# Second staging buffer for the expert-weight matrices, taken from the gather buffers and from the resident chunks

## Chip, core and metric

The kernel runs on one core of one Trainium2 chip. The metric is device microseconds (us) of one execution. All inputs, outputs and spilled intermediates lie in the chip's HBM; the work is fp32, in part split into two fp32r pieces that are multiplied separately.

## What is computed

One layer of a streaming encoder for 1024 prompt tokens and 64 sample tokens (with 512 cached positions for the latter). The part that matters here is the last one, a PEER layer with 16384 single-neuron experts. Each token picks 128 experts (8 heads of 16); `u` and `v` are tables of 16384 rows of 1024 floats:

```python
def peer_tokens(h, w_q, keys, u, v):
    q = (h @ w_q).reshape(T, PEER_HEADS, 2, PEER_D_KEY // 2)
    s = jnp.einsum('thcd,hcnd->thcn', q, keys)
    s1, i1 = lax.top_k(s[:, :, 0], PEER_TOPK)
    s2, i2 = lax.top_k(s[:, :, 1], PEER_TOPK)
    ...
    top, sel = lax.top_k(cand, PEER_TOPK)
    idx = jnp.take_along_axis(cidx, sel, axis=-1)
    g = jax.nn.softmax(top, axis=-1)
    act = jax.nn.gelu(jnp.einsum('td,thkd->thk', h, u[idx]), approximate=False)
    return jnp.einsum('thk,thkd->td', g * act, v[idx])
```

Ahead of it stand one wide projection, differential attention (8 heads), latent attention (16 heads), the branch projections and an output projection.

## The kernel before

The 1088 tokens are nine tiles of 128 (tile 8 holds the 64 sample tokens). Three groups of three tiles (`GROUPS`) go through projections and attention one after the other: group 0 from 0 to about 760 us of the profiled execution, group 1 to about 1865 us, group 2 to about 2960 us. After that comes a last stage without projections, up to the end.

The experts' work of a group runs beside the next group's projections and attention, in four kinds of jobs, written as Python generators:

- `route_job` (VectorE, mostly) finds the 128 experts of each token of a tile.
- `dots_job` fetches, for k = 0 to 127, row `u[idx[token, k]]` for all 128 tokens with one indirect DMA that GpSimd issues (L333, 512 KB into a tile of 4 KB per partition), and VectorE multiplies it with the token's row and sums (L358). These are the gathers; six tiles of 128 gathers each, 768 in all, run beside groups 1 and 2, and 320 in the last stage.
- `build_job` (tiles 0 to 6) turns indices and weights of a tile into a dense matrix of 128 tokens by 16384 experts. For 8 tokens at a time VectorE makes one-hot rows (L402, L403) and products (L411), ScalarE makes one product (L408), TensorE multiplies them (L418, into a PSUM tile "mm" that the projections use too, two buffers), and ScalarE copies 4 tokens' result out of PSUM into `stage` (L424). `stage` holds 16 tokens, 8 KB per partition, so four copies fill it; one DMA of 1 MB, issued on SyncE's queue (`ld`, L69, called at L426), then writes it to the tensor `Ad` in HBM. There is one buffer of that tile, in the pool `bp`: the next copy into it waits until that DMA has landed.
- `vgather_job` (tiles 8 and 7) gathers rows of `v` instead of using a dense matrix (192 gathers, L453), at the very end.

The last stage multiplies the dense matrices with the whole table `v` (L1206 and L1221) in two passes, tiles 0 to 2 and tiles 3 to 6, reading `Ad` back as `araw` in 16 chunks per tile. Of tile 6 (`TR`) the first `RC` = 9 chunks are never written to `Ad`: ScalarE copies them to the resident tile `Ares` (L422), and only the other 7 go through `stage`. Before that, `Ares` serves as scratch of the routing.

The order: `pump(us)` is called in the projections and attention with the time that the work just issued is thought to take, and advances the three queues of jobs at set rates ("r" route, "d" dots, "b" build; a dense build advances 4 tokens per step at `RATE_B` = 0.3 steps per us). This gives the program order; the scheduler of the tile framework then orders each engine's instructions by that priority on a simulated timeline, and places the semaphore waits. `behind` keeps the product of a gather (L358, L453) from being placed ahead of the VectorE instruction that preceded it in program order. Each engine executes its own list in order.

Gather buffers: the pool `gp` has `NGB` = 4 (tag "gb"). While `cur["more"]` is set, which is in groups 1 and 2 alone, three of every seven gathers go to another pool, `gm`, with three buffers, so that seven gathers can be on their way; in the last stage there are four. The pool `gm` also holds a small tile `cq`. In the last stage `cur["p2"]` is the pool for nearly everything, with `Ares` in it.

Of the kernel before, what the change touches and what calls it, by code (L numbers as in the profile page):

```python
# [10 lines left out]
F32 = mybir.dt.float32  # L11
# [9 lines left out]
D = 1024  # L21
# [19 lines left out]
NGB = 4  # L41
PB = 5
NB = 8
RC = 9
NWHOLE = 8
TR = 6
RATE_R2 = 0.41
# [12 lines left out]
def hybrid_tile(ctx: ExitStack, tc: tile.TileContext, A):  # L60
# [3 lines left out]
    def ld(out, in_):  # L64
        if out.dtype == F32R:
            out = out.bitcast(F32)
        if in_.dtype == F32R:
            in_ = in_.bitcast(F32)
        return SP.dma_start(out, in_)  # L69
# [34 lines left out]
    bp = ctx.enter_context(tc.tile_pool(name="bp", bufs=1))  # L104
# [9 lines left out]
    cur = {"gp": gp, "sm": sm, "ps": ps_mm, "more": None}  # L114
    gturn = [0]
# [207 lines left out]
    def drain(q, key=None):  # L323
        while key not in done and advance(q):
            pass

    def gather(src, idx):
        gturn[0] += 1
        if cur["more"] and gturn[0] % 7 % 2:
            gb = cur["more"].tile([128, D], F32, name="gm", tag="gm")  # L330
        else:
            gb = cur["gp"].tile([128, D], F32, name="gb", tag="gb")
        G.indirect_dma_start(out=gb, out_offset=None, in_=src, in_offset=bass.IndirectOffsetOnAxis(ap=idx, axis=0))  # L333
        return gb
# [4 lines left out]
    def dots_job(t):  # L339
        if t in GROUPS[-1]:  # L340
            drain("r", ("route", t))
        ns = 128 if t < 8 else 64
        eidx = bp.tile([128, 128], I32, name="beidx")
        gk = bp.tile([128, 128], F32, name="bgk", tag="bgk")
        h2 = bp.tile([128, D], F32, name="h2r")
        if t < 8:
            ld(eidx, eidxd[t])
            ld(gk, gkd[t])
            ld(h2, h2d[t * 128:t * 128 + 128])
        else:  # L350
            ld(eidx[:, :64], packed(eidxd[8]))
            ld(gk[:, :64], packed(gkd[8]))
            src = h2d[NP:]
            ld(h2, bass.AP(tensor=src.tensor, offset=src.offset, ap=[[0, 2], [D, 64], [1, D]]))
        act = bp.tile([128, 128], F32, name="act")
        for k in range(ns):
            gb = gather(A["peer_u"], eidx[:, k:k + 1])
            behind(V.scalar_tensor_tensor(gb, gb, 1.0, h2, op0=ALU.mult, op1=ALU.mult, accum_out=act[:, k:k + 1]))  # L358
            yield
        wgt = act  # L360
        S.activation(wgt[:, :ns], act[:, :ns], AF.Gelu)
        V.tensor_tensor(wgt[:, :ns], wgt[:, :ns], gk[:, :ns], op=ALU.mult)
        ld(wgtd[t, :, :ns], wgt[:, :ns])
        if t not in VGATHER:
            queues["b"].append((("build", t), build_job(t)))

    def build_job(t):
        if t == TR:
            drain("r")
        src = bp.tile([128, 3, 128], F32, name="bsrc", tag="oh1")  # L370
        ld(src[:, 0, :], wgtd[t])
        ld(src[:, 1:3, :], efd[t])
        p = cur["ps"].tile([128, 512], F32, name="mm")
        pv = p.rearrange("p (a n) -> p a n", n=128)
        for i in range(3):
            PE.transpose(pv[:, i, :], src[:, i, :], ident)
        ixT = bp.tile([128, 2, 128], BF16, name="ixT")
        S.copy(ixT, pv[:, 1:3, :])
        aT = bp.tile([128, 128], F32, name="aT")
        S.copy(aT, pv[:, 0, :])  # L380
        a3 = bp.tile([128, 3, 128], BF16, name="a3")
        a3f = bp.tile([128, 128], F32, name="a3f")
        for i in range(3):
            V.tensor_copy(a3[:, i], aT)
            if i == 0:
                V.tensor_copy(a3f, a3[:, 0])
            if i < 2:
                V.tensor_tensor(aT, aT, a3[:, i], op=ALU.subtract)
        yield
        shp = [128, 4, 128, 2]  # L390
        iv = iota2[:, None, :, :].to_broadcast(shp)

        def over(row, tt):
            return row[:, tt:tt + 8].rearrange("p (g x) -> p g x", x=2)[:, :, None, :].to_broadcast(shp)

        n = RC if t == TR else 0
        for t0 in range(0, 128, 16):
            stage = bp.tile([128, 16, 4, 8, 4], F32, name="stage", tag="stage")
            for tt in range(t0, t0 + 16, 8):
                oh1 = bp.tile(shp, BF16, name="oh1", tag="oh1")  # L400
                oh2 = bp.tile(shp, BF16, name="oh2")
                V.tensor_tensor(oh1, iv, over(ixT[:, 1], tt), op=ALU.is_equal)  # L402
                V.tensor_tensor(oh2, iv, over(ixT[:, 0], tt), op=ALU.is_equal)  # L403
                w3 = bp.tile([128, 3] + shp[1:], BF16, name="w3")
                for i in range(3):
                    if i == 0:
                        for x in range(8):
                            S.activation(w3[:, 0, x // 2, :, x % 2], oh2[:, x // 2, :, x % 2], AF.Copy,  # L408
                                         scale=a3f[:, tt + x:tt + x + 1])
                    else:  # L410
                        V.tensor_tensor(w3[:, i], oh2, over(a3[:, i], tt), op=ALU.mult)  # L411
                for q in range(2):
                    p = cur["ps"].tile([128, 512], F32, name="mm")
                    pv = p.rearrange("p (a n) -> p a n", n=128)
                    for j in range(4):
                        x = 4 * q + j
                        for i in range(3):
                            PE.matmul(pv[:, j, :], lhsT=oh1[:, x // 2, :, x % 2], rhs=w3[:, i, x // 2, :, x % 2],  # L418
                                      start=i == 0, stop=i == 2)
                    pc = p.rearrange("p (t c i) -> p c i t", t=4, i=8)  # L420
                    if n:
                        S.copy(cur["Ares"][:, :, (tt + 4 * q) // 4], pc[:, :n])  # L422
                    if n < 16:
                        S.copy(stage[:, n:, (tt - t0) // 4 + q], pc[:, n:])  # L424
                    yield
            ld(Ad[t, :, n:, t0 // 4:t0 // 4 + 4], stage[:, n:])  # L426
# [9 lines left out]
    def vgather_job(t):  # L436
        while "p2" not in cur:
            yield
        ns = 128 if t < 8 else 64
        eidx = bp.tile([128, 128], I32, name="beidx")  # L440
        wgt = bp.tile([128, 128], F32, name="vwgt", tag="bgk")
        acc = cur["p2"].tile([128, D], F32, name="gacc", bufs=1)
        if t < 8:
            ld(eidx, eidxd[t])
            ld(acc, x1d[t * 128:t * 128 + 128])
        else:
            ld(eidx[:, :64], packed(eidxd[8]))
            V.memset(acc[64:128], 0.0)
            ld(acc[0:64], x1d[NP:])
        ld(wgt[:, :ns], wgtd[t, :, :ns])  # L450
        for k in range(ns):
            gb = gather(A["peer_v"], eidx[:, k:k + 1])
            behind(V.scalar_tensor_tensor(acc, gb, wgt[:, k:k + 1], acc, op0=ALU.mult, op1=ALU.add))  # L453
            yield
        if t == 8:
            oth = cur["gp"].tile([128, D], F32, name="gb", tag="gb")
            ld(oth[0:64], acc[64:128])
            V.tensor_tensor(acc[0:64], acc[0:64], oth[0:64], op=ALU.add)
        if t == VGATHER[-1]:
            cur["late"] = lambda: finish(acc, tr(t), t)  # L460
        else:
            finish(acc, tr(t), t)
# [675 lines left out]
    p2 = ctx.enter_context(tc.tile_pool(name="p2", bufs=2, reuse_waits="tile"))  # L1138
    cur["p2"] = cur["sm"] = p2
    Ares = p2.tile([128, RC, 32, 8, 4], F32, name="Ares", bufs=1)  # L1140
    Af = Ares.rearrange("p c q i t -> p (c q i t)")
# [24 lines left out]
    for ip, tiles in enumerate(PASSES):  # L1166
# [11 lines left out]
        for c in range(16):  # L1178
# [15 lines left out]
            for t in tiles:  # L1194
                if t == TR and c < RC:
                    raw = Ares[:, c]
# [141 lines left out]
```

## Time and profile before

| | before |
|---|---|
| time, median of 3 runs | 4510.65 us (4497.69 to 4512.42) |
| profiled execution: its time | 4499.18 us |
| profiled execution: span from first to last instruction | 4497.4 us |
| TensorE busy | 3847.6 us (86%) |
| VectorE busy | 3203.9 us (71%) |
| ScalarE busy | 1603.3 us (36%) |
| GpSimd busy | 1942.8 us (43%) |
| DMA | 1183.10 MB, mean 263 GB/s |

How to read the rows below. PE is TensorE's matmuls, PEld its weight loads, DVE VectorE, ACT ScalarE, POOL GpSimd, SP SyncE (SPq its queue of DMAs). `gb<-in_peer_u` is a gather; L333 is a line of the kernel. In a view of stretches a row is one stretch: its bounds, its length, then busy time and number of instructions of PE, PEld, DVE, ACT and POOL, TensorE's granted clock as a share of full speed, the mean busy share of the 16 DMA engines, and GB/s; the last row sums the stretches. In a view of waits a row says which instruction's engine stood idle until what: us in total, times, longest. In a timeline a row is start, length, engine, line, operation, tiles, count, and in brackets the idle time before it and what ended it. In the chain of work that ended last, a piece is start, length and what it is; a DMA's piece runs from its issue to the end of the wait for its landing.

### The profile page before, as it was taken

What the parts mean: (1) busy time and instruction counts of PE and PEld (TensorE: products, weight loads), DVE (VectorE), ACT (ScalarE), POOL (GpSimd) and SP (SyncE); (2) the same over time, 40 slices, a digit from 0 to 9 for tenths busy, and PEclk for the clock granted to TensorE, in tenths of its full rate; (3) what the DMA queues carried; (4) which work ended last, traced back from release to release, by engine and by line L of the source; (5) the groups of instructions that cost most, each with busy time, mean ns of one, the idle gap of its engine ahead of it and who ended that gap; (6) DMA issues with size and microseconds to landing.
All of it is one profiled execution on the core that took longest, in us unless ns stands there. A gap on an engine that the chain in (4) does not pass through costs nothing.

```text
span 4497.4 us, 55226 instructions
## 1 busy us (share of the span) xinstructions
PE 3847.6 (86%) x18633; PEld 2898.2 (64%) x18633; DVE 3203.9 (71%) x7136; ACT 1603.3 (36%) x3656; POOL 1942.8 (43%) x1353
## 2 busy tenths in 40 slices
PE   6998988898788798887868877889999969999991
PEld 6977887556565565655546666654457858888881
DVE  4043457977788767797786777659847987777776
ACT  3344622025455513322454455133113532232320
POOL 3412241554456441143444656513434445545455
PEclk9967999987898898998778888989999979999995
DMA  5421244996777785697776767988868999989987
GB/s 176 168 96 56 67 170 169 352 350 231 267 263 269 272 320 216 226 329 290 245 248 239 256 239 253 351 291 311 320 246 317 349 328 332 351 312 352 321 314 260
DMA packets 467587, 1183.10 MB, mean 263 GB/s; under 512 B 45352, under 2 KB 218888, under 8 KB 452584
## 3 DMA queue, kind: packets, MB, share of 16 engines
q0 software_dynamic: 184320, 671.17, 41.4%
q1 hardware_dynamic: 282984, 508.41, 32.3%
q8 instruction: 147, 2.41, 0.2%
q14 instruction: 136, 1.11, 0.1%
HBM read 1074.60 MB, written 104.56 MB: 262 GB/s over the span
## 4 chain that ended last, share of the span: by engine, by line
PE 42%; DMA 13%; DVE 13%; issue 5%; ACT 4%; POOL 2%; SPq 0%; another core or an unknown queue 0%; ACTq 0%; POOLq 0%; DVEq 0%
PE acc_ps L1221 16%; PE mm L167 9%; PE acc_ps L1206 5%; DMA Ad<-stage 4%; DMA gb<-in_peer_v,beidx 3%; DVE gb L358 3%; DMA gb<-in_peer_u,beidx 2%; PE mm L418 2%; DVE gm L358 2%; POOL gb L333 2%; PE mm L827 2%; PE sc L795 1%; PE mm L952 1%; PE sc L793 1%; ACT w L408 1%
## 5 line engine op out<-in xcount | busy, mean ns | idle before, releaser
L333 POOL DMA_INDIRECT gb<-in_peer_u,beidx x758 | 1028.2, 1356 | 1364.7 <-DVE gb L358 811.1
L358 DVE SCALAR_TENSOR_TENSOR gb<-gb,h2r 128x1024 f32<-128x1024 f32 x758 | 918.3, 1220 | 174.4 <-DMA gb<-in_peer_u,beidx 157.9
L333 POOL DMA_INDIRECT gm<-in_peer_u,beidx x330 | 429.9, 1303 | 501.4 <-DVE gm L358 274.6
L1221 PE MATMUL acc_ps<-vhi,ahi 128*128 128x512 f32 x1408 | 439.9, 395 | 23.4 <-ACT ahi L1214 23.4
L1221 PE MATMUL acc_ps<-vhi,alo 128*128 128x512 f32 x1408 | 444.1, 396 | 3.0 <-DVE alo L1215 3.0
L1221 PE MATMUL acc_ps<-vlo,ahi 128*128 128x512 f32 x1408 | 441.0, 395 | 0.0
L358 DVE SCALAR_TENSOR_TENSOR gm<-gm,h2r 128x1024 f32<-128x1024 f32 x330 | 402.1, 1218 | 24.0 <-DMA gm<-in_peer_u,beidx 21.4
L333 POOL DMA_INDIRECT gb<-in_peer_v,beidx x192 | 268.0, 1396 | 229.7 <-DVE gacc L453 150.1
L167 PE MATMUL mm<-h,wraw 128*128 128x384 f32 (+1 forms) x1024 | 325.5, 479 | 20.4 <-ACT qd L739 10.4
L1206 PE MATMUL acc_ps<-vw,aw 128*128 128x512 f32 x768 | 335.0, 596 | 1.4 <-ACT aw L1202 1.4
L418 PE MATMUL mm<-w,oh 128*128 128x128 bf16 x2688 | 231.0, 237 | 111.5 <-DVE oh L402 50.5
L1221 PEld LDWEIGHTS acc_ps<-vhi,ahi 128*128 128x128 f32 x1408 | 265.6, 189 | 85.5 <-ACT ahi L1214 23.6
L453 DVE SCALAR_TENSOR_TENSOR gacc<-gb,vwgt,gacc 128x1024 f32<-128x1024 f32 x192 | 246.2, 1282 | 93.3 <-DMA gb<-in_peer_v,beidx 88.1
L1221 PEld LDWEIGHTS acc_ps<-vhi,alo 128*128 128x128 f32 x1408 | 265.0, 189 | 63.9 <-DVE alo L1215 3.7
L1221 PEld LDWEIGHTS acc_ps<-vlo,ahi 128*128 128x128 f32 x1408 | 265.5, 189 | 60.2 <-DVE vlo L1192 0.2
L408 ACT ACTIVATE w<-oh,a3f 128x128 bf16<-128x128 bf16 x896 | 280.8, 429 | 54.0 <-DVE oh L403 24.3
L179 POOL TENSOR_TENSOR wlo<-wraw,whi 128x2048 fp32r<-128x2048 f32 (+1 forms) x42 | 186.8, 4447 | 260.6 <-ACT whi L178 255.0
L418 PEld LDWEIGHTS <-oh 128*128 128x128 bf16 x2688 | 191.9, 106 | 160.6 <-issue 73.2
L167 PEld LDWEIGHTS mm<-h,wraw 128*128 128x128 f32 x1024 | 201.0, 199 | 133.8 <-issue 11.4
L167 PE MATMUL mm<-wraw,h 128*128 128x256 f32 (+1 forms) x960 | 235.6, 402 | 37.7 <-ACT vt L720 27.8
L1206 PEld LDWEIGHTS acc_ps<-vw,aw 128*128 128x128 f32 x768 | 145.5, 191 | 179.1 <-issue 175.6
L1214 ACT CAST ahi<-araw 128x1024 fp32r<-128x1024 f32 x79 | 82.8, 1049 | 474.4 <-PE acc_ps L1221 395.7
(384 smaller groups left out, 7574.2 us busy)
## 6 DMA issues: line engine op xcount, KB each, us to landing
vraw<-in_peer_v SPq DMA_DIRECT2D x192, 512.0 KB
wraw<-in_w_in SPq DMA_DIRECT2D x66, 1024.0 KB
araw<-Ad SPq DMA_DIRECT2D x103, 512.0 KB
Ad<-stage SPq DMA_DIRECT2D x48, 1024.0 KB
vw<-in_peer_v SPq DMA_DIRECT2D x64, 512.0 KB
wraw<-in_w_a SPq DMA_DIRECT2D x12, 1024.0 KB
wraw<-in_w_b SPq DMA_DIRECT2D x12, 1024.0 KB
wraw<-in_w_out SPq DMA_DIRECT2D x12, 1024.0 KB
```

The costliest lines, as they stand in the source:

```text
L167: PE.matmul(out, lhsT=L[0], rhs=R[0], start=start, stop=stop)
L179: G.tensor_tensor(lo[:, :n], raw[:, :n], hi[:, :n].bitcast(F32), op=ALU.subtract)
L333: G.indirect_dma_start(out=gb, out_offset=None, in_=src, in_offset=bass.IndirectOffsetOnAxis(ap=idx, axis=0))
L358: behind(V.scalar_tensor_tensor(gb, gb, 1.0, h2, op0=ALU.mult, op1=ALU.mult, accum_out=act[:, k:k + 1]))
L408: S.activation(w3[:, 0, x // 2, :, x % 2], oh2[:, x // 2, :, x % 2], AF.Copy, scale=a3f[:, tt + x:tt + x + 1])
L418: PE.matmul(pv[:, j, :], lhsT=oh1[:, x // 2, :, x % 2], rhs=w3[:, i, x // 2, :, x % 2], start=i == 0, stop=i == 2)
L453: behind(V.scalar_tensor_tensor(acc, gb, wgt[:, k:k + 1], acc, op0=ALU.mult, op1=ALU.add))
L793: PE.matmul(ps[:nq, a:b], lhsT=Q[:, c, qc:qc + nq], rhs=K[:, c, a - o:b - o], start=True, stop=False)
L827: PE.matmul(po[:nq, :128], lhsT=PT[:kw, b, :nq], rhs=Vt[:kw, b, :], start=b == 0, stop=b == nb - 1)
L1206: PE.matmul(pst[t][:, ds], lhsT=rv[:, i, :], rhs=vb[i][:, ds], start=c == 0 and i == 0, stop=False)
L1214: S.copy(av, rv)
L1221: PE.matmul(pst[t][:, ds], lhsT=L[:, i, :], rhs=R[:, ds], start=c == (0 if ip else NWHOLE and -1) and i == 0 and L is ahi and R is vb[i][0 ...
```

## The change

The matrices' `stage` tile gets a second buffer of 16 tokens: every other block of 16 tokens is staged in a tile of the pool `gm` (in groups 1 and 2) or of the pool `p2` (in the last stage), the others in `bp` as before, each pool with one buffer. Its 8 KB per partition are found by leaving one gather buffer in `gm` instead of three (each 4 KB), so that five gathers instead of seven can be on their way in groups 1 and 2, one of five going to `gm`; and in `p2` by keeping 7 chunks of tile 6 resident instead of 9 (each 4 KB).

```diff
-RC = 9
+RC = 7
...
     def gather(src, idx):
         gturn[0] += 1
-        if cur["more"] and gturn[0] % 7 % 2:
-            gb = cur["more"].tile([128, D], F32, name="gm", tag="gm")
+        if cur["more"] and gturn[0] % 5 == 1:
+            gb = cur["more"].tile([128, D], F32, name="gm", tag="gm", bufs=1)
         else:
             gb = cur["gp"].tile([128, D], F32, name="gb", tag="gb")
...
         n = RC if t == TR else 0
         for t0 in range(0, 128, 16):
-            stage = bp.tile([128, 16, 4, 8, 4], F32, name="stage", tag="stage")
+            sp = (cur["more"] or cur["p2"]) if t0 % 32 else bp
+            stage = sp.tile([128, 16, 4, 8, 4], F32, name="stage", tag="stage", bufs=1)
```

## Rows read from the trace of the kernel before

**Rows 1.** The page's first part: busy time, share of the span, instructions

```profile
PE 3847.6 (86%) x18633; PEld 2898.2 (64%) x18633; DVE 3203.9 (71%) x7136; ACT 1603.3 (36%) x3656; POOL 1942.8 (43%) x1353
```

**Rows 2.** Groups 1 and 2, stretches 760 to 1865 and 1865 to 2960 us: their sum

```profile
sum 2200.00, PE 1798.61 PEld 1303.29 DVE 1706.54 ACT 848.90 POOL 1022.99; mean PE 899.30 PEld 651.65 DVE 853.27 ACT 424.45 POOL 511.50
```

**Rows 3.** Waits from 760 to 2960 us

```profile
POOL gb L333 <- DVE gb L358: 437.8, 100, 39.9
POOL gm L333 <- DVE gm L358: 274.6, 61, 18.5
...
ACT stage L424 <- DMA Ad<-stage: 130.2, 28, 15.4
ACT stage L424 <- PE mm L418: 116.6, 62, 7.9
```

**Rows 4.** The chain of work that ended last, 760 to 2960 us, by line

```profile
by line: PE mm L167 19.0%; DMA Ad<-stage 7.5%; issue 7.0%; DVE gb L358 5.7%; DVE gm L358 3.9%; PE mm L827 3.4%; PE mm L418 2.9%; PE sc L795 2.8%; PE mm L952 2.5%; PE sc L793 2.4%; DMA gb<-in_peer_u,beidx 2.3%; ACT w L408 2.1%; PE tp L758 1.
```

**Rows 5.** SyncE's timeline: issues of two stage DMAs of one build

```profile
1170.69 0.52 SPq L69 DMA_DIRECT2D Ad<-stage  x1
1202.35 0.53 SPq L69 DMA_DIRECT2D Ad<-stage  x1
```

**Rows 6.** TensorE's timeline, 1198 to 1240 us

```profile
1220.77 1.44 PE L418 MATMUL mm<-w,oh 128*128 128x128 bf16 x12 [7.59 <-ACT stage L424]
```

**Rows 7.** 29 stretches in which ACT waits for a stage DMA, to 2960 us

```profile
1204.71:1220.13 15.42, 8.47 (x36) 4.93 (x35) 9.69 (x17) 0.00 (x1) 8.04 (x7) 0.84 1.04 389
...
sum 135.13, PE 76.36 PEld 53.77 DVE 96.04 ACT 0.07 POOL 58.92; mean PE 2.63 PEld 1.85 DVE 3.31 ACT 0.00 POOL 2.03
```

**Rows 8.** The 8 us behind each of those 29 stretches

```profile
sum 232.00, PE 191.60 PEld 140.60 DVE 142.24 ACT 126.42 POOL 80.80; mean PE 6.61 PEld 4.85 DVE 4.90 ACT 4.36 POOL 2.79
```

**Rows 9.** Pieces of the chain in groups 1 and 2

```profile
1202.35 17.68 DMA Ad<-stage
...
2581.39 6.04 DMA gm<-in_peer_u,beidx
...
2836.74 19.43 DMA gm<-in_peer_u,beidx
```

**Rows 10.** Line L358, 760 to 2960 us: instructions, and idle time before them

```profile
L358 DVE SCALAR_TENSOR_TENSOR gb<-gb,h2r x438: 1199/1218/1344, 768.7 to 2945.8; 128x1024 f32<-128x1024 f32 x146
...
L358 DVE SCALAR_TENSOR_TENSOR gm<-gm,h2r x330: 1175/1218/1348, 766.3 to 2947.0; 128x1024 f32<-128x1024 f32 x165
...
  DMA gb<-in_peer_u,beidx: 40.0, 33
  DMA gm<-in_peer_u,beidx: 21.4, 24
```

**Rows 11.** Line L358, 3130 to 4000 us, likewise

```profile
L358 DVE SCALAR_TENSOR_TENSOR gb<-gb,h2r x297: 1197/1219/1349, 3130.5 to 3991.4; 128x1024 f32<-128x1024 f32 x149
...
  DMA gb<-in_peer_u,beidx: 111.6, 87
```

**Rows 12.** Line L453, likewise

```profile
L453 DVE SCALAR_TENSOR_TENSOR gacc<-gb,vwgt,gacc 128x1024 f32<-128x1024 f32 x192 | 246.2, 1282 | 93.3 <-DMA gb<-in_peer_v,beidx 88.1
```

**Rows 13.** 59 stretches in which DVE waits for a gather, 760 to 2960 us

```profile
sum 62.74, PE 51.70 PEld 34.85 DVE 0.15 ACT 11.76 POOL 40.19; mean PE 0.88 PEld 0.59 DVE 0.00 ACT 0.20 POOL 0.68
```

**Rows 14.** DMA issues of the page: count and size

```profile
araw<-Ad SPq DMA_DIRECT2D x103, 512.0 KB
...
Ad<-stage SPq DMA_DIRECT2D x8, 448.0 KB
```

**Rows 15.** Stage waits from 2960 to 3130 us

```profile
  DMA Ad<-stage: 33.3, 3
```

**Rows 16.** Stretches of the last stage

```profile
2960.00:3130.00 170.00, 154.95 (x617) 82.33 (x616) 135.24 (x582) 61.16 (x149) 32.27 (x27) 0.90 0.83 289
3660.00:3990.00 330.00, 304.71 (x1302) 246.86 (x1303) 251.30 (x372) 83.04 (x82) 179.77 (x129) 0.95 0.90 331
4400.00:4450.00 50.00, 0.00 (x0) 0.00 (x0) 35.42 (x56) 2.30 (x4) 27.95 (x23) 0.53 0.82 279
```

## The prediction

> **What bounds the kernel now.** The page comes first: TensorE is the busiest engine at 86% [rows 1], so what is to be gained lies where TensorE stands still and something else decides. The stretches of groups 1 and 2 show it: over 2200 us TensorE is busy 1798.61 us, 81.8%, while VectorE has 1706.54 us [rows 2]. No engine is full there; each waits for another in turn. In the last stage TensorE is nearer its limit (304.71 of 330 us in one stretch [rows 16]), and from 4400 us on it has no work at all: the end is a run of gathers of `v` with their products on VectorE [rows 16].
>
> The waits of groups 1 and 2 are read next. ScalarE stands 130.2 us, 28 times, before a copy into `stage` until the stage's previous contents have landed in HBM [rows 3]. The reader should see that this wait stands in an in-order queue: evictions of projections, exponentials and the copies of transposes are queued behind that copy. The chain of work that ended last gives the stage's DMA 7.5% of these 2200 us, 165 us, as the second largest line [rows 4]. A place shows how: the third DMA of a build was issued at 1202.35 [rows 5], landed 17.68 us later [rows 9], ScalarE waited 15.42 us of it [rows 7], and TensorE, whose "mm" buffers were both full, 7.59 us [rows 6].
>
> **The gain, step by step.** With two buffers, block n waits for the DMA of block n-2. Two issues in a row stand 31.66 us apart (1170.69 and 1202.35 [rows 5]); the landing took 17.68 us there, and that is among the longest waits. So a DMA has landed before its buffer is wanted again, and I take the 28 waits as gone. What is late next in their place is the copy's own input: 62 times ScalarE already waits for TensorE's L418 (116.6 us [rows 3]), since these matmuls are queued among the projections'. That wait stays.
>
> What the end gets from it is not ScalarE's 130 us but TensorE's loss. I cut the trace into the 29 stretches in which ScalarE waits so (135.13 us together; the view of waits counts 28). TensorE is busy 76.36 us in them [rows 7], where its usual share of 81.8% would make 110.5. It loses 34.1 us. In the 8 us behind each it is busy 191.60 of 232.00 us, 82.6% [rows 8], which is 1.8 us above its usual share: little is caught up. Gain: 34.1 - 1.8 = 32 us. Bounds: 0, if TensorE's holes only move to the next wait; 135 us, if all of ScalarE's waiting comes off the chain, which gave it more weight (165 us) than TensorE's holes do. I take 32 because TensorE is the engine with most work in these groups and its holes are counted, not inferred.
>
> **What five gather buffers cost.** GpSimd issues gather k once the product of gather k-7 (after: k-5) is done; it does nothing else in these groups, so only gathers queue behind that wait, and then VectorE's products, with the row maxima, splits and one-hot rows behind them. There are 438 + 330 = 768 gathers in 2181 us (766.3 to 2947.0) [rows 10], one each 2.84 us. With seven buffers a gather has six intervals, 17.0 us, to be issued and to land; with five, four intervals, 11.4 us. The chain shows landings between 6.04 and 19.43 us from issue [rows 9]. So the usual gather still comes in time and the late ones no longer do.
>
> How much VectorE then waits the trace doesn't show; its two neighbours do. With seven buffers it waits 40.0 + 21.4 = 61.4 us for 768 gathers [rows 10], 0.08 us each. With four, in the last stage, 111.6 us for 297 [rows 11] and 88.1 us for 192 [rows 12], 0.41 us each. Five lies between; a third of the way up from four on a scale of ratios it is 0.24 us, 184 us in all, 123 us more than now. At four buffers' price it would be 253 us more, at seven's none.
>
> What does such a wait cost TensorE? In the 59 stretches of it, 62.74 us, TensorE is busy 51.70 us, 82.4% [rows 13], no less than usual: these waits are short and cost nothing. The other bound is ScalarE's waits, which cost TensorE 34.1 of 135.13 us, 25%. Longer waits for gathers will lie between; as their nearest row is the first, I take 10%: 123 x 0.10 = 12 us. Bounds: 0 and 253 x 0.25 = 63 us.
>
> The Trainium skill gives the time of one such DMA as about 2.0 us plus the bytes at 436 GB/s ("DMA: Bandwidth & Descriptors", Anatomy of one DMA); by it I estimate 3.2 us for 512 KB, and this term of the sum would be 0. The trace doesn't agree: 6.04 us and more, with the DMA engines shared.
>
> **Seven resident chunks.** Two more chunks of tile 6 go through HBM. That adds 2 loads of `araw` to 103, 512 KB each, and makes each of the 8 small stage DMAs 576 KB instead of 448 [rows 14]: 1.0 + 1.0 MB. The loads join SyncE's queue in the second pass, between loads of `v`. ScalarE's copies out of PSUM stay as many and as long in sum (the same 512 columns, split otherwise). The 2.1 MB cost nothing on TensorE, which runs ahead of the gathers there; they share the DMA engines, 0.90 busy at 331 GB/s [rows 16], with the gathers that make the end. Bounds 0 and 2.1 MB / 331 GB/s = 6 us; so near to full I take 4.
>
> **From 2960 to 3130 us** ScalarE waits 33.3 us for the stage's DMA [rows 15], but TensorE is busy 154.95 of 170 us, so at most 15 us is to be had; 91% busy is nearer to nothing, and I take 4. It cancels the 4 above.
>
> **Moved work.** The stage's DMA is issued on SyncE's queue when the copies are done, now a little earlier; the loads queued behind it start earlier too. No instruction is added in the groups. What the scheduler's order does beyond that is not to be read from this trace; I put it at 0 and into the range.
>
> Sum against the profiled execution: 4499.18 - 32 + 12 + 4 - 4 = 4479 us, 20 us less. That execution lies 11.5 us below the median of 4510.65, against which the change will be judged: 4490 us. The last stage starts after group 2 and keeps its own length, so what the groups give is carried to the end.
>
> **Rivals.**
>
> *Slower: the ring of gathers is what is scarce.* GpSimd stands 437.8 + 274.6 = 712 us in the groups until VectorE frees a buffer [rows 3], and the change takes two away. If the waits rise to four buffers' 0.41 us, 253 us more, and each costs TensorE as much as ScalarE's do, that is 63 us: 4499 - 32 + 63 = 4530, by the median 4542. It decides from the point where the cost passes 32 us: 13% of 253 us, or 26% of the 123. For it: VectorE is 78% busy and holds the row maxima of attention, so it has little room. Against it: GpSimd's waits are those of an engine that runs ahead, and rows 13.
> The Trainium skill says that repeating gaps on the engine that should be saturated can mean too few buffers ("Perfetto Trace Analysis", Identifying Performance Opportunities). By that rule this rival gains if GpSimd is that engine; at 43% busy [rows 1] it isn't.
>
> *No change: the hole moves.* While ScalarE waits, the DMA engines are full (1.04 in the 15.42 us stretch [rows 7]). The bytes stay, and TensorE then waits for L418's inputs or weights instead. Gain 0 to 15 us: 4495 to 4515 by the median. Against it: rows 8 show no queue of other waits right behind.
>
> *Much faster: the chain is right.* All of 135 us comes off, less 12: 4376 on the profiled execution, 4388 by the median. For it the 165 us of rows 4; against it TensorE's 56% in rows 7, work that has to be done anyway.
>
> **How the numbers follow.** About 0.3% (13.5 us) is what a measurement of this kernel can tell from no change. The forecast (4455 to 4510) has 0.5, of which 0.36 lies more than 13.5 us below the median. The much faster case, from 4455 down, has 0.11; no change 0.14; slower 0.25. So faster 0.47, same 0.28, slower 0.25. The range leaves out the far half of the fast case and the end of the slow one, about 0.13: 4435 to 4555.
>
> **What would show it.** Right: ScalarE's wait for the stage's DMA almost gone from groups 1 and 2; TensorE's busy share there above 81.8%; the last gather of group 2 earlier than 2947 us by some 20 us; VectorE's waits for gathers between 61 and 250 us, with TensorE working through them; the last stage as long as before. Wrong: TensorE's share in the groups unchanged although the stage's waits are gone (the hole moved), or a group longer with VectorE's waits for gathers above 250 us and TensorE idle in them (the ring was scarce), or a last stage that is longer by more than 10 us.

## The result, and the profile after

The changed kernel took 4438.53 us, median of 4 runs (4432.13 to 4445.65), against 4507.77 us of the kernel before (4 runs): a ratio of 0.985 with a 95% interval of 0.9825 to 0.9875, or 69 us less. It is faster, as forecast, and inside the range, but by more than three times the size: the forecast was 20 us.

The page's first part, to be held against [rows 1]:

```profile
PE 3806.9 (86%) x18633; PEld 2863.9 (65%) x18633; DVE 3201.9 (72%) x7136; ACT 1605.9 (36%) x3656; POOL 1906.1 (43%) x1353
```

The profiled execution took 4432.13 us, 67 us less than that of before. TensorE and GpSimd are busy some 40 us less each, with the instruction counts of before. Line numbers from the change on are higher by one: L424 is L425 now, L418 is L419.

To see where the time went, both traces are cut at the same work: the end of the last product of queries with the experts' keys (`sc<-keysT,q`, L1111, L1112 after) of groups 0, 1 and 2, and the end of the execution. Stretches of before: group 1, group 2, last stage.

```profile
702.10:1757.00 1054.90, 880.17 (x4190) 629.61 (x4190) 833.81 (x2034) 386.34 (x1006) 489.76 (x384) 0.87 0.79 284
1757.00:2970.20 1213.20, 980.97 (x5165) 728.13 (x5165) 911.77 (x2190) 478.25 (x1257) 534.71 (x384) 0.85 0.75 261
2970.20:4497.00 1526.80, 1373.61 (x5767) 991.80 (x5766) 1180.32 (x2149) 443.76 (x687) 701.66 (x512) 0.94 0.87 316
```

And of after:

```profile
705.60:1738.60 1033.00, 867.65 (x4190) 618.15 (x4190) 830.65 (x2015) 384.55 (x1003) 469.60 (x384) 0.88 0.82 290
1738.60:2896.50 1157.90, 951.51 (x5166) 703.67 (x5165) 913.96 (x2208) 481.74 (x1260) 506.25 (x384) 0.86 0.79 274
2896.50:4430.00 1533.50, 1372.62 (x5767) 990.94 (x5766) 1179.37 (x2149) 444.73 (x687) 713.62 (x512) 0.94 0.87 316
```

Group 1 is 22 us shorter and group 2 55 us; the last stage is 7 us longer. The two groups together went from 2268.1 to 2190.9 us. TensorE's idle time in them fell from 407.0 to 371.7 us, by 35; its *busy* time fell from 1861.2 to 1819.2 us, by 42, with the same number of matmuls (9355 and 9356). The granted clock says how that can be: it rose by 0.01 in each group, so matmuls took less time. A row of one line, with the same number of columns throughout, shows the two levels of that clock (minimum, median and maximum duration in ns, projections of `h`, after):

```profile
L167 PE MATMUL mm<-wraw,h x909: 379/379/797, 701.7 to 1905.3; 128*128 128x256 f32 x150, 128*64 128x256 f32 x32
```

379 is the shortest and the median, 797 the longest, 2.1 times as long. From the rows' clocks, TensorE stood at 1.2 GHz for an estimated 638 us of the two groups before and 572 after (twice the missing share times the length; two decimals make each good to some 20 us, their difference to some 30). The time at 2.4 GHz is about equal, 1630 and 1619 us. By this estimate 66 of the 77 us gained are time at the low clock. That is a way of counting and not yet a cause: the half stages below lose 42 us of idle time, and by the same reckoning only some 12 us of low clock.

Waits from 700 to 2960 us after, to be held against [rows 3, 10]:

```profile
POOL gb L333 <- DVE gb L358: 547.1, 181, 15.5
ACT stage L425 <- PE mm L419: 158.6, 99, 9.1
...
POOL gm L333 <- DVE gm L358: 115.5, 48, 11.8
...
DVE gb L358 <- DMA gb<-in_peer_u,beidx: 79.1, 71, 5.1
...
DVE gm L358 <- DMA gm<-in_peer_u,beidx: 32.6, 29, 5.5
```

ScalarE's wait for the stage's DMA has no row here any more. On TensorE the rows of waits for ScalarE's copies into `stage` sum to 66.9 us before and 9.1 us after; the largest of them, before first, then after:

```profile
PE mm L167 <- ACT stage L424: 36.3, 15, 7.7
```

```profile
PE mm L167 <- ACT stage L425: 6.1, 7, 2.0
```

That is 58 us less, of which 35 remain in the idle time: TensorE waits more for others. ScalarE's wait for TensorE's products is what is late next, 158.6 us for 116.6. GpSimd waits 663 us for VectorE in these two rows, 712 before. VectorE waits 111.7 us for gathers, 61.4 before.

The chain of work that ended last, groups 1 and 2, to be held against [rows 4]:

```profile
by line: PE mm L167 18.5%; issue 14.5%; DMA gb<-in_peer_u,beidx 6.6%; DVE gb L358 6.1%; POOL gb L333 4.0%; PE sc L796 2.8%; PE mm L828 2.6%; DMA gm<-in_peer_u,beidx 2.4%; PE sc L794 2.4%; PE mm L419 2.0%; DVE gm L358 1.7%; PE tp L759 1.7%; 
```

The stage's DMA, 165 us before, isn't among the lines. "Issue", time in which an engine waited for nothing that the profile shows, doubled from 7.0 to 14.5%, and the gathers into `gb` went from 2.3 to 6.6%. So most of what the chain had given to the stage's DMA was taken over by others.

### The profile page after: what moved, and what is told of

Same layout as the page of the kernel before. It is cut to its first block, busy times and chain, and to the rows that moved or that the text cites. A ratio compares the mean times of both kernels' runs of the same rounds, so it can differ in the third digit from the quotient of the medians.

```text
span 4430.4 us, 55267 instructions
## 1 busy us (share of the span) xinstructions
PE 3806.9 (86%) x18633; PEld 2863.9 (65%) x18633; DVE 3201.9 (72%) x7136; ACT 1605.9 (36%) x3656; POOL 1906.1 (43%) x1353
## 4 chain that ended last, share of the span: by engine, by line
PE 39%; DVE 13%; DMA 12%; issue 9%; POOL 4%; ACT 2%; SPq 0%; ACTq 0%; POOLq 0%; DVEq 0%
PE acc_ps L1222 16%; PE mm L167 9%; PE acc_ps L1207 5%; DMA gb<-in_peer_u,beidx 4%; DVE gb L358 4%; POOL gb L333 3%; DMA gb<-in_peer_v,beidx 3%; PE mm L419 2%; PE sc L796 1%; PE mm L828 1%; DMA gm<-in_peer_u,beidx 1%; PE sc L794 1%; DVE w L412 1%; DVE gm L358 1%; PE tp L759 1%
## 5 line engine op out<-in xcount | busy, mean ns | idle before, releaser
L333 POOL DMA_INDIRECT gb<-in_peer_u,beidx x934 | 1211.2, 1297 | 1534.8 <-DVE gb L358 921.0
L358 DVE SCALAR_TENSOR_TENSOR gb<-gb,h2r 128x1024 f32<-128x1024 f32 x934 | 1127.3, 1220 | 211.6 <-DMA gb<-in_peer_u,beidx 191.5
L333 POOL DMA_INDIRECT gb<-in_peer_v,beidx x192 | 280.1, 1459 | 221.1 <-DVE gacc L454 132.5
L333 POOL DMA_INDIRECT gm<-in_peer_u,beidx x154 | 198.2, 1287 | 305.9 <-DVE gm L358 115.5
L419 PE MATMUL mm<-w,oh 128*128 128x128 bf16 x2688 | 227.7, 235 | 79.7 <-DVE oh L403 47.6
L419 PEld LDWEIGHTS <-oh 128*128 128x128 bf16 x2688 | 188.8, 105 | 129.0 <-DVE oh L403 62.0
L1191 ACT CAST vhi<-vraw 128x1024 fp32r<-128x1024 f32 x192 | 200.4, 1052 | 106.5 <-PE acc_ps L1222 51.3
```

What stands on the lines that cost most here:

```text
L1191: S.copy(hi, raw)
```

## The experiments

The theories at the start, in the order in which they came up: that the stage's wait itself was the cost, worth more than its holes in TensorE; that the shorter ring of gathers gave part of the gain by itself (fewer gathers in flight beside other transfers); and that the new order of instructions, which the scheduler makes anew for every edit, moved the time whatever the buffers do. Times are medians; each ratio is against runs of the kernel before made beside them (medians 4513.38, 4514.06 and 4513.29 us; the last on a second chip, as are the runs at the rate 0.29 below and, at 0.31, the ring alone and the half stages). The ratio is not exactly the quotient of the medians; the two differ by up to 8 us.

**The ring alone.** Against before:

```diff
-        if cur["more"] and gturn[0] % 7 % 2:
-            gb = cur["more"].tile([128, D], F32, name="gm", tag="gm")
+        if cur["more"] and gturn[0] % 5 == 1:
+            gb = cur["more"].tile([128, D], F32, name="gm", tag="gm", bufs=1)
```

> The kernel before with the five gather buffers alone (one stage buffer, nine resident chunks). Theory A (the gain is the stage's wait, in TensorE's holes and in the lower clock behind them; the ring only costs): 4508 to 4540 us, VectorE's waits for gathers in groups 1 and 2 rise from 61 to 100-190 us, ScalarE's wait for the stage DMA stays near 130 us, and TensorE's time at the lower clock there stays at about 630 us. Theory B (fewer gathers in flight leave the DMA engines to the other transfers, and that is part of the gain): 4470 to 4495 us. Theory C (any new order of the instructions moves the time by tens of us): either way, with no relation to these waits.

4523.63 us, ratio 1.0023 (1.0001 to 1.0046): 10 us slower, as Theory A had it. So the shorter ring gives nothing by itself. Two details missed: ScalarE's wait for the stage rose to 150.5 us, and the time at the low clock, reckoned as above, is 670 us and not 630. Groups 1 and 2 of its profile, the waits in them, and the sums over the stretches in which VectorE waits for a gather (98) and ScalarE for the stage (28):

```profile
702.60:1803.80 1101.20, 888.57 (x4190) 637.10 (x4190) 838.37 (x2058) 385.61 (x1006) 476.66 (x384) 0.86 0.77 272
1803.80:3009.60 1205.80, 965.52 (x5166) 715.48 (x5165) 908.55 (x2166) 478.36 (x1257) 509.69 (x384) 0.85 0.75 263
```

```profile
POOL gb L333 <- DVE gb L358: 642.5, 191, 19.5
ACT stage L424 <- DMA Ad<-stage: 150.5, 28, 16.8
...
DVE gb L358 <- DMA gb<-in_peer_u,beidx: 85.6, 67, 5.0
...
DVE gm L358 <- DMA gm<-in_peer_u,beidx: 31.1, 27, 5.8
```

```profile
sum 119.09, PE 85.78 PEld 62.78 DVE 0.26 ACT 31.40 POOL 75.24; mean PE 0.88 PEld 0.64 DVE 0.00 ACT 0.32 POOL 0.77
```

```profile
sum 150.51, PE 69.19 PEld 47.35 DVE 101.00 ACT 0.07 POOL 58.22; mean PE 2.47 PEld 1.69 DVE 3.61 ACT 0.00 POOL 2.08
```

This execution, 4538.87 us, is the second longest of ten (4510.84 to 4539.67), so its sums stand for more than the median's 10 us. TensorE idles 452.9 us, 46 more than before. In the gather waits it is busy 72.0%, in its groups as a whole 80.4%: 10 us lost. In the stage's waits it now loses 52 us (150.51 x 0.804 - 69.19), 34 before. So of the 46 us, 10 are lost in the gather waits and 18 more in the stage's, which got longer here; the rest lies elsewhere. At the rate 0.31 below, the stage's wait does not get longer with the shorter ring (93.2 us for 105.4), and TensorE idles 48 us more all the same.

**The change without its last stage.** Against before, with the ring of five as above, and nine resident chunks:

```diff
-            stage = bp.tile([128, 16, 4, 8, 4], F32, name="stage", tag="stage")
+            sp = (cur["more"] or bp) if t0 % 32 else bp
+            stage = sp.tile([128, 16, 4, 8, 4], F32, name="stage", tag="stage", bufs=1)
```

> The change without its part in the last stage: second stage buffer and five gather buffers in groups 1 and 2, nine resident chunks and one stage buffer behind them. Theory A: the groups end where they end after the change (2896 us), and the last stage is as long as before it (1527 us instead of 1534): 4430 us, 0 to 10 us below the changed kernel. Theory B the same. Theory C: 4400 to 4480 us.

4434.93 us, 0.9812 (0.9786 to 0.9837), as expected. The gain is all in the groups. (The profiled execution, 4450.17 us, is the longest of its four; its groups end at 2921.2 us and not at 2896.) Its last stage has the length of before to the tenth:

```profile
2921.20:4448.00 1526.80, 1372.89 (x5766) 989.17 (x5766) 1180.38 (x2149) 443.93 (x687) 699.83 (x512) 0.94 0.87 316
```

against 1533.50 us of the change. The medians differ by 4 us, within their noise.

**Two half stages, all seven gather buffers.** The old tile's 8 KB are cut into two tiles of 8 tokens, each with a DMA of its own; no memory is taken from anything:

```diff
-        for t0 in range(0, 128, 16):
-            stage = bp.tile([128, 16, 4, 8, 4], F32, name="stage", tag="stage")
-            for tt in range(t0, t0 + 16, 8):
+        for t0 in range(0, 128, 8):
+            stage = bp.tile([128, 16, 2, 8, 4], F32, name="stage", tag="stage%d" % (t0 // 8 % 2))
+            for tt in range(t0, t0 + 8, 8):
...
-            ld(Ad[t, :, n:, t0 // 4:t0 // 4 + 4], stage[:, n:])
+            ld(Ad[t, :, n:, t0 // 4:t0 // 4 + 2], stage[:, n:])
...
```

(Not shown: group 0's scratch, which used the old `stage` tile, is split in the same way.)

> The kernel before with its 8 KB of stage cut into two buffers of 8 tokens, seven gather buffers and nine resident chunks kept; the DMA to HBM then writes runs of 256 bytes instead of 512. Theory A: the wait for landing shrinks if a half stage (512 KB) lands within one half's interval of some 13 us, and the kernel gains 30 to 70 us: 4440 to 4480 us; it gains nothing if the short runs double the landing time, and ScalarE's wait then stays above 100 us. Theory B: no gain, 4508 us, since the ring is as before. Theory C: either way.

4453.52 us, 0.9856 (0.9812 to 0.9899): 60 us less, with an interval of 46 to 85, from the wait alone. That is Theory A's range. Its groups, and its waits:

```profile
701.50:1740.40 1038.90, 882.38 (x4191) 634.00 (x4190) 837.34 (x2062) 387.60 (x1008) 485.19 (x384) 0.87 0.82 289
1740.40:2928.00 1187.60, 979.19 (x5165) 725.85 (x5165) 906.82 (x2161) 481.87 (x1257) 528.82 (x384) 0.85 0.79 267
```

```profile
ACT stage L424 <- PE mm L418: 155.1, 85, 10.6
...
ACT stage L424 <- DMA Ad<-stage: 18.2, 3, 8.4
```

The stage's wait is down to 18.2 us, 3 times (12.2 us of it in the groups), TensorE's waits for copies into `stage` to 22.6 us in sum, and its idle time to 364.9 us, 42 less than before. Its busy time hardly moved in this execution; but this execution's clock, 0.894, is the lower half of its four (0.892 to 0.901, from 4470.12 to 4430.82 us).

**Rings of six, five and four beside two full stages.** For a sixth buffer room was made by loading a table of cosines per group instead of once, and by one buffer for `kp` instead of two; the ring of five was run with the same edits. All three leave the last stage as it was before; the ring of four is the change without its last stage, with no gather in `gm`.

```diff
-        if cur["more"] and gturn[0] % 5 == 1:
-            gb = cur["more"].tile([128, D], F32, name="gm", tag="gm", bufs=1)
+        if cur["more"] and gturn[0] % 3 == 1:
+            gb = cur["more"].tile([128, D], F32, name="gm", tag="gm", bufs=2)
...
+        cs = att.tile([128, 3, 2, 16], F32, name="cs", bufs=1)
+        ld(cs, A["cossin"][:, tiles[0]:tiles[0] + 3])
```

> As the run without the last stage's part, with six gather buffers instead of five (room made by loading the rotary table for each group by itself and by one buffer less for the small rotary key tile). Theory A: the ring costs a little, so 0 to 15 us faster than with five: 4415 to 4432 us. Theory B: 10 us slower or more: 4440 us and above. Theory C: no order among four, five and six.

> The run with two stage buffers and six gather buffers, with five gather buffers again and its other two edits (rotary table by group, one small key tile) kept. Theory A2 (six buffers are no worse than five; the 25 us between those two runs are TensorE's clock and the order of the instructions): within 15 us of the run with six, 4445 to 4475 us, with a granted clock near 0.891. Theory B (more gathers in flight cost): 4435 us, as with five buffers before.

> Two stage buffers in groups 1 and 2 and only four gather buffers there; nine resident chunks. Theory A (the ring costs through VectorE's waits): these waits rise from 132 us to 250-320 us, TensorE's idle time in groups 1 and 2 rises from 376 us by 40 to 100 us, and the time is 4470 to 4530 us. Theory B: not slower than five buffers, 4435 us or less. Theory C: idle time and VectorE's waits unrelated.

Six: 4460.02 us, 0.9878 (0.9852 to 0.9904). Five: 4434.97, 0.9835 (0.9785 to 0.9884). Four: 4483.35, 0.9951 (0.9932 to 0.997). Groups 1 and 2 of the three, in this order:

```profile
sum 2228.00, PE 1852.46 PEld 1352.96 DVE 1745.08 ACT 866.33 POOL 1026.15; mean PE 926.23 PEld 676.48 DVE 872.54 ACT 433.17 POOL 513.08
```

```profile
sum 2203.00, PE 1818.33 PEld 1326.30 DVE 1745.15 ACT 866.65 POOL 982.75; mean PE 909.16 PEld 663.15 DVE 872.58 ACT 433.32 POOL 491.38
```

```profile
sum 2224.00, PE 1799.77 PEld 1318.07 DVE 1744.75 ACT 867.48 POOL 962.69; mean PE 899.88 PEld 659.03 DVE 872.38 ACT 433.74 POOL 481.34
```

Six buffers are no better than five, and four are clearly worse. The six missed Theory A's 4415 to 4432 us, and the five missed Theory A2's 4445 to 4475 and came where Theory B, that more gathers in flight cost, had put them. As a general rule B doesn't hold, since four are slower than five; for six against five, 25 us apart with four runs each, it stays open. These two have nearly equal idle time on TensorE (375.5 and 384.7 us) and differ in its busy time, 1852 and 1818 us, and in the mean granted clock of their runs, 0.891 and 0.900. Four came in Theory A's range; VectorE's waits, 230.5 us, are more than the 184 that the prediction took for five, and less than Theory A's 250 to 320:

```profile
POOL gb L333 <- DVE gb L358: 752.2, 329, 14.0
DVE gb L358 <- DMA gb<-in_peer_u,beidx: 230.5, 166, 6.4
```

**The order.** `RATE_B`, the rate at which the builds are handed out between the other work, changes the program order and nothing else:

```diff
-RATE_B, RATE_B2 = 0.3, 0.5
+RATE_B, RATE_B2 = 0.31, 0.5
```

It was applied to the kernel before, the change, the ring of five alone and the two half stages, and with 0.29 to the first two.

> The kernel before, with the rate of dense builds 0.31 instead of 0.30 steps per us: a change of order with no meaning of its own. Theory A: 4500 to 4520 us, ScalarE's wait for the stage DMA 110 to 150 us. Theory C (any new order moves the time by tens of us, and the change's 69 us are of that kind): outside of that, by 30 us or more.

> The changed kernel, with the rate of dense builds 0.31 instead of 0.30. Theory A: 4425 to 4455 us, and the pair before/after at this rate 55 to 85 us apart. Theory C: 4470 us or more, or a pair less than 40 us apart.

> Five gather buffers alone, one stage buffer, nine resident chunks, at the build rate 0.31 (beside the kernel before at 0.31, 4489 us). Theory A (the ring costs some 10 us in TensorE's idle time, whatever the order): 4490 to 4520 us; ScalarE's wait for the stage DMA 90 to 150 us; VectorE's waits for gathers 100 to 150 us. Theory C (order): 25 us or more away from 4499.

> Two stage buffers of 8 tokens, seven gather buffers, at the build rate 0.31. Theory A (with the wait gone TensorE's idle time in groups 1 and 2 falls by 30 to 45 us whatever the order): idle time 350 to 370 us beside 398, and a time of 4430 to 4465 us. Theory C: no fall of the idle time, or a time within 15 us of 4489.

> The kernel before at the build rate 0.29, a third order of its instructions. Theory A: 4485 to 4525 us, ScalarE's wait for the stage DMA 100 to 150 us. Theory C: spread wider than that.

> The changed kernel at the build rate 0.29. Theory A (a gain of some 30 to 75 us at every order, 50 in the mean): 30 to 75 us below the kernel before at 0.29. Theory C: within 25 us of it, on either side.

| medians, us | 0.29 | 0.30 | 0.31 |
|---|---|---|---|
| before | 4495.22 | 4507.77 to 4514.06 | 4489.26 |
| the change | 4447.02 | 4438.53 | 4460.44 |
| the ring of five alone | | 4523.63 | 4528.02 |
| two half stages, ring of seven | | 4453.52 | 4420.40 |

Against before at the same rate the change is worth 48, 69 and 29 us; the mean is 49. The 29 us are near the noise: the two intervals against before at 0.30 overlap (0.9918 to 0.9968 for the kernel before, 0.9839 to 0.9936 for the change). The order alone moves each of the two by some 20 us between its ends, more than the 13.5 us that the prediction took for what a measurement tells from nothing. The sign holds at all three rates, so the order isn't the cause of the gain; but it holds some 20 of the 69 us. Nor does the gain follow the wait that goes: ScalarE's wait for the stage is 172.6, 130.2 and 105.4 us in the kernel before at the three rates.

Of the six expectations, those for the rate 0.29 were met in their times, though the wait of 172.6 us is longer than the 100 to 150 expected. At 0.31 all four times missed Theory A: the kernel before and the half stages were faster, the change and the ring alone slower. The pair, 29 us apart, meets Theory C's mark (under 40), and so does the ring alone, 29 us from 4499 (25 or more). So at this rate the order counts as much as Theory C said.

At 0.31 the parts are: the wait alone 69 us off, the ring alone 39 us on; together 30, and the change measured 29. At 0.30 they are 60 off and 10 on, together 50 and not 69. By the ratios the wait alone is worth 65 us at 0.30 and 60 at 0.31, so nothing tells these two apart. Group stretches at 0.31 of the kernel before and of the half stages:

```profile
704.40:1749.90 1045.50, 872.75 (x4191) 626.67 (x4190) 834.18 (x2034) 386.77 (x1006) 492.48 (x384) 0.88 0.80 287
1749.90:2966.20 1216.30, 990.53 (x5165) 733.24 (x5165) 911.77 (x2190) 479.86 (x1257) 535.33 (x384) 0.84 0.74 260
```

```profile
704.10:1733.50 1029.40, 867.59 (x4190) 626.95 (x4190) 832.86 (x2031) 386.43 (x1005) 489.85 (x384) 0.89 0.83 291
1733.50:2878.00 1144.50, 948.04 (x5165) 705.49 (x5165) 910.43 (x2192) 479.34 (x1257) 542.69 (x384) 0.87 0.82 277
```

TensorE's idle time falls from 398.5 to 358.3 us, its busy time from 1863.3 to 1815.6. ScalarE's wait for the stage falls from 105.4 us (25 times) to 41.2 (4 times). The stretches of it in the kernel before at 0.31 (26, cut as those of [rows 7]), in sum:

```profile
sum 108.65, PE 52.25 PEld 35.09 DVE 75.59 ACT 0.07 POOL 37.85; mean PE 2.01 PEld 1.35 DVE 2.91 ACT 0.00 POOL 1.46
```

The version with two half stages, seven gather buffers and nine resident chunks at 0.31, 4420.4 us and 0.9811 (0.9785 to 0.9836), is the fastest median of all and takes no memory; its interval touches that of the change.

## Why the prediction was right in sign and wrong in size

**The wait goes: right.** Ready before it is wanted again, the stage's DMA is waited for no more. The last product of a gather in group 2 starts at 2881.2 us, 2947.0 before [rows 10], and TensorE's busy share of the two groups rose from 82.1 to 83.0%.

**"Gain: 34.1 - 1.8 = 32 us": the term that was mis-sized.** It measured 60 us at one rate and 69 at the other, by the two half stages. The part of it that the step counted was counted well: with the wait all but gone at 0.30 and more than halved at 0.31, TensorE idles 42 us less at 0.30, where the holes came to 34 [rows 7], and 40 us less at 0.31, where by the same reckoning they come to 37 (108.65 x 0.824 - 52.25). What the sum left out is the clock, which makes the same matmuls shorter or longer: with the same 9355, TensorE's busy time fell by 42 us in the change and by 48 in the half stages at 0.31. (In the profiled pair of the half stages at 0.30 it did not fall; there the clock's part rests on the medians.) The step took TensorE's busy share as its work. The 8 us behind each stage wait, where [rows 8] gave it 82.6% busy, have rows like these:

```profile
1178.67:1186.67 8.00, 2.21 (x10) 1.88 (x11) 5.74 (x13) 4.33 (x12) 0.58 (x1) 0.50 0.96 390
1220.13:1228.13 8.00, 7.36 (x26) 4.79 (x26) 2.59 (x4) 3.55 (x10) 0.00 (x0) 0.67 0.62 257
...
2663.53:2671.53 8.00, 7.19 (x23) 4.75 (x23) 3.11 (x6) 3.73 (x11) 0.12 (x1) 0.50 0.47 194
```

7.36 us busy at a clock of 0.67 is work of about 5 us. The mean clock of the 29 rows is 0.78, where the two groups have 0.86, and in the 16 us that follow each it is 0.91. Over these 16 us TensorE is busy thus:

```profile
sum 464.00, PE 394.53 PEld 291.04 DVE 381.35 ACT 215.09 POOL 206.48; mean PE 13.60 PEld 10.04 DVE 13.15 ACT 7.42 POOL 7.12
```

That is 85%, and at the higher clock: part of what the holes cost is made good there, so these stretches don't settle the price. The medians give it from another side. The mean clock of all runs rose from 0.8904 to 0.8958 with the half stages, and at 0.31 from 0.8919 to 0.8990. Among the half stages' own runs 0.009 of clock goes with 39 us, 4.4 us for 0.001. So the clock is worth an estimated 24 and 31 us, with the idle time 66 and 71; measured were 60 and 69. That is a sum that fits, not a proof that the two are separate: lines through the runs of the other kernels give 0.9 to 5.2 us for 0.001, which would make it 5 to 28 and 6 to 37 us. The bound of 135 us, and with it the range, held this.

The Trainium skill says that the array runs at half its clock after it has been idle, and that activity lifts it ("TensorE: Matmul & The Clock Gate", What's actually happening). The 0.78 right behind the waits and the 0.91 later agree. But the holes alone don't set the clock: the ring of four has the most idle time of all the kernels with two stages, 424.2 us, and the least busy time, 1799.8. Why the clock is higher in one order of the work than in another is not settled, and so isn't why six buffers were slower than five. And some 20 of the 69 us hang on the order, which the prediction had put at 0: at 0.31 the change gained 29.

**"123 x 0.10 = 12 us": right at 0.30 by luck, too small at 0.31.** VectorE's waits for gathers came to 111.7 us in the change and 116.7 with the ring alone, where 184 were taken; a ring of four has 230.5 where 315 would follow from 0.41 us each. So the scale gave 1.4 to 1.6 times what was measured. The price failed the other way: 55 us more of such waits came with 46 us more idle time on TensorE in the ring alone, and at 0.31 with 48 us more (2289.2 - 1842.8 = 446.4, for 398.5). But little of that is lost while VectorE waits. In the ring alone it was 10 us at 0.30, and at 0.31 nothing: 117.5 us of waits, in which TensorE is busy 80.9%, for 80.5% of its groups. The step priced only these stretches; what it had itself put behind them, VectorE's row maxima and splits, it left unpriced. One wait of TensorE at the start of attention in group 2 shows it: for the split queries `Qd` (L147, on VectorE). Before, the change, the ring alone at 0.31, and the change at 0.31:

```profile
PE sc L795 <- DVE Qd L147: 13.3, 1, 13.3
```

```profile
PE sc L796 <- DVE Qd L147: 24.3, 1, 24.3
```

```profile
PE sc L795 <- DVE Qd L147: 42.0, 1, 42.0
```

```profile
PE sc L796 <- DVE Qd L147: 45.6, 1, 45.6
```

The kernel before and the half stages at 0.31, with seven buffers, have no such row. So at 0.31 this one wait is about as long as all that the shorter ring added. From the start of group 2 up to it VectorE had waited 17.9 us for gathers in the ring alone at 0.31, and 2.2 us in the kernel before at 0.31 up to its own first `Qd`; whether the rest of the 42 us comes from the ring or from the new order isn't shown. In the change itself, in the 103 stretches of it, TensorE is busy 78.9%:

```profile
sum 112.06, PE 88.44 PEld 61.62 DVE 0.25 ACT 24.89 POOL 67.53; mean PE 0.86 PEld 0.60 DVE 0.00 ACT 0.24 POOL 0.66
```

The groups have 83.0%, so 5 us are lost there. Against the half stages with their seven buffers, the change has 7 us more of TensorE's idle time at 0.30 (371.7 for 364.9) and 43 more at 0.31 (401.0 for 358.3). How much of the bound of 63 is paid hangs on the order. The sum of the two groups of the change at 0.31, from which the 401.0 is taken:

```profile
sum 2230.20, PE 1829.17 PEld 1335.93 DVE 1746.46 ACT 866.35 POOL 994.87; mean PE 914.59 PEld 667.97 DVE 873.23 ACT 433.17 POOL 497.44
```

**"Bounds 0 and 6 us; I take 4": near.** The last stage is 7 us longer, just past the bound, with TensorE's busy time equal; the medians with and without it are 4 us apart. One stretch shows where; before first, then after:

```profile
3670.20:4170.20 500.00, 484.91 (x2081) 393.31 (x2082) 384.76 (x481) 134.97 (x132) 271.68 (x195) 0.98 0.90 332
```

```profile
3596.50:4096.50 500.00, 481.27 (x2069) 390.33 (x2070) 382.70 (x479) 132.22 (x129) 265.02 (x192) 0.98 0.90 331
```

In the same 500 us 12 matmuls and 3 gathers fewer are done, with the DMA engines at 0.90 both times. That fits added loads taking the gathers' place, as the prediction had it. **The 4 us from 2960 to 3130 us** didn't come: the stage's wait is gone there too, but in the first 200 us of the last stage TensorE does 741 matmuls, and 742 before.

**The rivals.** *Slower* fell: the ring's cost, 10 and 39 us, stayed below the wait's worth at both rates. It is real, though, and at 0.31 more than half of that worth; a ring of four gives back 48 us of the gain (4483.35 for 4434.93). The Trainium skill's remark that repeating gaps on the engine that should be saturated can mean too few buffers ("Perfetto Trace Analysis", Identifying Performance Opportunities) agrees if it is read on TensorE, whose waits for copies into `stage` fell from 66.9 to 9.1 us. The size of the waits alone would have sent one to GpSimd, with 712 us; but two gather buffers were worth 10 to 39 us there, and the 130 us that ScalarE waited for the stage 60 to 69. *No change* fell at 0.30, where TensorE's idle time fell by 35 us. At 0.31 half of it is true: the change's idle time is 401.0 us for 398.5 before, the stage's holes gone and the wait for `Qd` in their place; the 29 us come with 34 us less busy time. With the half stages the hole did not move at either rate. *Much faster* fell short: of the chain's 165 us, 60 to 69 came off.

## What to carry to other kernels

A wait of a lightly used engine is priced by what the busiest engine loses in it, and those holes can be counted in the trace; but busy time is work only at a known clock, so count it with the granted clock of the stretch, behind the wait too. And a wait that costs nothing while it lasts can be paid for later, where the busiest engine waits for what was queued behind it. To hide a transfer behind its buffer, first cut the buffer in two: half the size twice did as much here as the whole size twice, which had to pay with two gather buffers, and took no memory. Before a gain of one per cent is credited to an edit in a kernel that a scheduler orders, move a harmless parameter that changes the order alone, in both versions.

## What was not expected of the hardware

The same 9355 matmuls of the two groups took from 1800 to 1863 us of busy time in different kernels that do the same work. Executions of one and the same program differ by 39 us with their mean granted clock (0.892 to 0.901 in the half stages), which is more than most of the edits here. And a stage DMA of half the size, in runs half as long, landed early enough most of the time: 3 waits instead of 28 at 0.30, 4 instead of 25 at 0.31.
